# Gated heads of a hybrid encoder step: decays from a running sum along the free dimension, and a packed first stage

## The chip, the cores and the metric

One core of a Trainium2 chip runs the whole program: TensorE (PE, matmuls, with PEld for its weight loads), VectorE (DVE), ScalarE (ACT), GpSimd (POOL) and SyncE (SP, which issues most DMAs). The metric is the device time of one execution in microseconds (us); the median of the runs is compared.

## The reference, cut to what matters

One step of a two-layer encoder for 256 prompt tokens and 32 sample tokens that share the weights (T = 288 columns in all). Layer 0 mixes with four retention heads and four gated heads (GLA), layer 1 with attention; each is followed by a convolution FFN. The change touches the gated heads and the beginning of the program.

```python
z = jnp.einsum('btd,de->bte', h, w_in).astype(f32)          # h = rmsnorm(x)
qa, ka, va, ga, qb, kb, vb, gb, lo = jnp.split(z, cuts, axis=-1)
...
log_a = (jax.nn.log_sigmoid(lo @ gate_w2 + gate_b) / GLA_GATE_TAU).reshape(B, T, H_GLA, DK_GLA)
...
def gla_chunk(S, q, k, v, log_a):
    b = jnp.cumsum(log_a, axis=1)
    diff = b[:, :, None] - b[:, None, :]
    w = jnp.where(causal, jnp.exp(jnp.where(causal, diff, 0.0)), 0.0)
    scores = jnp.einsum('bihd,bjhd,bijhd->bhij', q, k, w)
    o = jnp.einsum('bhij,bjhv->bihv', scores, v)
    o = o + jnp.einsum('bihd,bhdv->bihv', q * jnp.exp(b), S)
    b_last = b[:, -1]
    S_new = jnp.exp(b_last)[..., None] * S + jnp.einsum('bjhd,bjhv->bhdv', k * jnp.exp(b_last[:, None] - b), v)
    return S_new, o
```

The gate has rank 16 (`lo`), 4 heads of 128 features, and a divisor of 16 under the exponent.

## The kernel before

**Layout and matmuls.** Features lie on the 128 partitions and the 288 tokens along the free dimension, so an activation of 2048 features is 16 tiles of 128 x 288. Weights and activations are f32; each is split into a rounded part and a rest (`wh`, `wl`, `xh`, `xl`), and a product is three matmuls (L81 to L83: high by high, high by low, low by high). One input product (`input_product`, L76) is 16 k-tiles times three matmuls, 48 of 288 columns, into one PSUM tile `acc` (four of them). Its weights come in two halves of 128 x 1024 (512 KB) on SP's queue (L58), four such buffers `w`; ScalarE casts each half (L59), VectorE subtracts (L60), three buffers each. Small matmuls use four PSUM tiles `mm`.

**Order.** A framework orders the instructions: each engine gets its own in-order list, filled by priority (program order) and by what the planner holds ready. So an instruction may run ahead of others that stand before it in the code, on engines that have nothing ready; on the chip every engine then works through its list in order.

**Start** (`start`, L244). `first_project` (L85) loads x in four pieces and the key weights of gated head 0 in two, all on SP's queue; per k-tile `gain_in` (L137) makes `xh` on ScalarE and `xl` on VectorE, and three matmuls follow. Then come the low-rank product (L254 to L266: weights of 16 columns, split by ScalarE and VectorE into one padded 128-column tile, 32 matmuls) and the query product of head 0. x's squares are summed meanwhile (L101); `norm_stat` (L158) turns the sums into R, the reciprocal root mean square of every token, spread over all partitions (L162 to L188: six tiny matmuls, a chain of small VectorE and ScalarE operations, six more matmuls). R is multiplied into every product when it leaves PSUM.

**Gates** (`gates`, L424). Tokens on partitions: three matmuls of the scaled `lo` (33 rows, the last for the bias) with the gate weights, 512 columns, f32; then Abs, Exp and Ln on ScalarE (L433 to L437), a minimum and subtraction on VectorE (L439), and a split into `la` (L440). They run after the first value product v0 of head 0.

**A gated head** (`gla_head`, L465). k, q, v0, v1 and two gate products z0, z1 (head 0 has k and q from the start). Scores inside the chunk are built in seven levels (128, 64, ... 2): at each level the second half of a block looks back at the first, with decays counted to the middle of the block. The decays of all levels and of the chunk ends are sums over `log_a`: L487 multiplies `la` (128 tokens x 128 features) with `lvl`, a constant 0/1 matrix per level, in 14 matmuls per head and five PSUM tiles, and ScalarE takes the Exp from PSUM into E (128 x 9 x 288, one buffer; L493 to L507). Then VectorE multiplies k and q by E (L525), small matmuls form the masked scores (L536), VectorE merges them (L545, L564), and outputs, states and the head's norm follow (L569 to L596). Heads are chained so that the next head's products fill TensorE between the small matmuls (`chain`, L227). `lvl` is loaded once on SP's queue and rounded (L409 to L413).

**Memory.** Pool "in" holds x and the low-rank weights during the start; pools "b" (36,928 bytes a partition) and "ab" (everything of the mixer) are opened after it and take its place, b first, from the same address on.

## Time and profile before

| what | us |
|---|---|
| median of 3 runs (2724.24 to 2726.68) | 2724.97 |
| the profiled execution | 2725.65 |
| its span, first to last instruction | 2723.9 |
| TensorE busy | 2699.6 |
| VectorE busy | 1559.9 |
| ScalarE busy | 1118.2 |
| GpSimd busy | 117.9 |

The span is what the trace shows; the time of the execution has 1.75 us around it. Busy time of PE counts overlapping matmuls once, and a matmul's end is modelled; where two matmuls follow each other without a wait, the distance of their starts is what one costs. In a timeline row stand start, duration, engine, line, operation, the tiles (written <- read), the shapes, the count of merged instructions, and in brackets how long the engine had been idle before and what released it. A row of a group has busy time, mean duration in ns, and idle time before its instructions.

### The profile page before, as it was taken

Reading aid. Unit: us, or ns where it says so; the run is one execution under the profiler, and the core shown is the slowest. Engines: PE = TensorE matmul, PEld = TensorE weight load, DVE = VectorE, ACT = ScalarE, POOL = GpSimd, SP = SyncE. Lnnn points to the kernel's source line nnn. Section 1 sums busy time; section 2 is a strip of 40 time slices with the busy share of each in tenths; the row PEclk is TensorE's granted clock in tenths of the full one; section 3 lists DMA queues with packets and bytes.
Section 4 is the critical chain, followed back from the end, with each engine's and each line's share of the span. In section 5 each row is a group of like instructions: output and inputs, shape, how many; then the busy total and the mean of one; then the engine's idle time right before and its main releaser. Section 6 shows DMA issues by size and latency. Waiting matters only on the chain.

```text
span 2723.9 us, 48869 instructions
## 1 busy us (share of the span) xinstructions
PE 2699.6 (99%) x20240; PEld 2667.4 (98%) x20240; DVE 1559.9 (57%) x2496; ACT 1118.2 (41%) x1494; POOL 117.9 (4%) x428
## 2 busy tenths in 40 slices
PE   8999999999999999999999999999999999999998
PEld 7999999999999999999999999999999999999998
DVE  5566555666665446666555555556666544666544
ACT  7444344443333333434444444444433333433443
POOL 1000000000000000000001110000000000000000
PEclk9999999999999999999999999999999999999999
DMA  5344444555555555555556555544555555555554
GB/s 197 117 134 137 155 155 151 192 163 166 167 165 163 167 171 164 169 164 164 166 174 205 186 184 169 164 158 163 169 164 168 162 165 171 166 167 165 164 167 130
DMA packets 126911, 448.81 MB, mean 165 GB/s; under 512 B 15866, under 2 KB 16186, under 8 KB 126688
## 3 DMA queue, kind: packets, MB, share of 16 engines
q1 hardware_dynamic: 119664, 427.15, 49.5%
q0 software_dynamic: 6880, 18.50, 2.1%
q8 instruction: 158, 2.59, 0.4%
q14 instruction: 65, 0.53, 0.1%
q10 hardware_dynamic: 144, 0.04, 0.0%
HBM read 435.22 MB, written 10.40 MB: 164 GB/s over the span
## 4 chain that ended last, share of the span: by engine, by line
PE 98%; ACT 1%; DVE 1%; DMA 0%; issue 0%; SPq 0%; DVEq 0%; ACTq 0%
PE acc L82 31%; PE acc L83 31%; PE acc L81 31%; PE mm L536 1%; DMA w<-in_w_in 0%; PE mm L382 0%; PE mm L659 0%; ACT wh L59 0%; PE mm L748 0%; PE mm L712 0%; ACT L493 0%; PE mm L660 0%; DVE wl L60 0%; PE mm L649 0%; PE mm L185 0%; PE mm L487 0%
## 5 line engine op out<-in xcount | busy, mean ns | idle before, releaser
L59 ACT CAST wh<-w 128x1024 fp32r<-128x1024 f32 (+1 forms) x816 | 844.3, 1035 | 1484.4 <-PE acc L82 1205.0
L60 DVE TENSOR_TENSOR wl<-w,wh 128x1024 fp32r<-128x1024 f32 (+1 forms) x816 | 980.6, 1202 | 747.7 <-ACT wh L59 747.3
L81 PE MATMUL acc<-xh,wh 128*128 128x288 f32 x4480 | 1323.3, 295 | 8.1 <-ACT wh L59 8.1
L83 PE MATMUL acc<-xh,wl 128*128 128x288 f32 x4480 | 1324.3, 296 | 1.3 <-DVE wl L60 1.3
L82 PE MATMUL acc<-xl,wh 128*128 128x288 f32 x4480 | 1324.7, 296 | 0.0
L81 PEld LDWEIGHTS acc<-xh,wh 128*128 128x128 f32 x4480 | 844.0, 188 | 11.9 <-ACT wh L59 8.4
L83 PEld LDWEIGHTS acc<-xh,wl 128*128 128x128 f32 x4480 | 843.2, 188 | 2.8 <-DVE wl L60 2.1
L82 PEld LDWEIGHTS acc<-xl,wh 128*128 128x128 f32 x4480 | 843.8, 188 | 2.0 <-issue 1.0
L82 PE MATMUL acc<-bl,wh 128*128 128x288 f32 x1920 | 566.0, 295 | 0.0
L83 PE MATMUL acc<-bh,wl 128*128 128x288 f32 x1920 | 565.6, 295 | 0.0
L81 PE MATMUL acc<-bh,wh 128*128 128x288 f32 x1920 | 563.6, 294 | 0.4 <-ACT wh L59 0.4
L81 PEld LDWEIGHTS acc<-bh,wh 128*128 128x128 f32 x1920 | 360.8, 188 | 1.5 <-ACT wh L59 0.6
L82 PEld LDWEIGHTS acc<-bl,wh 128*128 128x128 f32 x1920 | 360.8, 188 | 0.1
L83 PEld LDWEIGHTS acc<-bh,wl 128*128 128x128 f32 x1920 | 360.5, 188 | 0.2 <-issue 0.2
L312 DVE SCALAR_TENSOR_TENSOR gc<-gp,convp,gc 128x290 f32<-128x290 f32 x176 | 91.3, 519 | 3.2
L318 DVE TENSOR_TENSOR v<-acc,R 128x288 f32<-128x288 f32 x88 | 40.2, 457 | 87.8 <-PE acc L83 87.8
L303 DVE TENSOR_TENSOR gp<-acc,R 128x256 f32<-128x256 f32 x88 | 37.4, 425 | 88.4 <-PE acc L83 88.4
L305 POOL COPY conv_out<-gp 128x2 f32<-128x2 f32 x88 | 16.2, 185 | 1309.0 <-DVE gp L303 1309.0
L116 ACT CAST bh<-v 128x288 fp32r<-128x288 f32 x88 | 38.1, 433 | 14.6 <-DVE v L320 14.6
L310 DVE TENSOR_SCALAR gc<-gp,convp 128x290 f32<-128x290 f32 x88 | 38.0, 431 | 10.2 <-POOL conv_out L306 0.9
L319 DVE TENSOR_TENSOR v<-v,sg 128x256 f32<-128x256 f32 x88 | 37.4, 425 | 9.2
L117 DVE TENSOR_TENSOR bl<-v,bh 128x288 fp32r<-128x288 f32 x88 | 39.7, 451 | 0.7 <-ACT bh L116 0.7
(254 smaller groups left out, 1098.6 us busy)
## 6 DMA issues: line engine op xcount, KB each, us to landing
w<-in_w_ffn_up SPq DMA_DIRECT2D x352, 512.0 KB, 3.8
w<-in_w_ffn_down SPq DMA_DIRECT2D x128, 512.0 KB, 3.7
w<-in_w_in SPq DMA_DIRECT2D x112, 512.0 KB, 3.8
w<-in_w_qkv SPq DMA_DIRECT2D x96, 512.0 KB, 3.8
w<-in_w_ffn_down SPq DMA_DIRECT2D x64, 384.0 KB, 3.2
w<-in_w_out_ab SPq DMA_DIRECT2D x32, 512.0 KB, 3.9
w<-in_w_out_att SPq DMA_DIRECT2D x32, 512.0 KB, 3.8
x<-in_xT SPq DMA_DIRECT2D x4, 576.0 KB, 5.7
```

The lines of the kernel that those rows point to most:

```text
L59: nc.scalar.copy(h, w)
L60: nc.vector.tensor_tensor(l, w, h.bitcast(F32), op=ALU.subtract)
L81: nc.tensor.matmul(ps, lhsT=h, rhs=xh, start=first, stop=False)
L82: nc.tensor.matmul(ps, lhsT=h, rhs=xl, start=False, stop=False)
L83: nc.tensor.matmul(ps, lhsT=l, rhs=xh, start=False, stop=last)
L116: self.nc.scalar.copy(h, v)
L117: self.nc.vector.tensor_tensor(l, v, h.bitcast(F32), op=ALU.subtract)
L303: nc.vector.tensor_tensor(gp[:, 2 : TP + 2], g[:, :TP], self.R[:, :TP], op=ALU.mult)
L310: nc.vector.tensor_scalar(gc, gp[:, 0:W], cw[:, 0:1], cw[:, 3:4], op0=ALU.mult, op1=ALU.add)
L312: nc.vector.scalar_tensor_tensor(gc, gp[:, w : w + W], cw[:, w : w + 1], gc, op0=ALU.mult, op1=ALU.add)
L318: nc.vector.tensor_tensor(v, u, self.R, op=ALU.mult)
L319: nc.vector.tensor_tensor(v[:, :TP], v[:, :TP], s[:, :TP], op=ALU.mult)
```

## The change

1. **Gates with features on partitions.** `gates` multiplies the gate weights (as the stationary operand, 128 columns per head) with `lo`: four matmuls of 288 columns, in two groups, head 0 first and then heads 1 to 3, each group with its own Abs, Exp, Ln and subtraction. A `tensor_tensor_scan` per group forms running sums along the tokens; `keep` is 1 except for 0 at tokens 0, 128 and 256, where the sum starts anew.
2. **Decays from differences.** In each gated head, the 14 matmuls with `lvl` and the Exp from PSUM go. VectorE forms, per level, (sum at the middle) - (sum) for first halves and (sum) - (sum at the middle) for second halves, and three differences to the ends of the token blocks; ScalarE takes Exp(x/16) from E to E in five calls.
3. **Packed first stage.** x, the key and query weights of head 0 and the low-rank weights are packed by k-tile into one array (128 x 16 x 560) and loaded in nine chunks (1, 1, then 2 k-tiles each) on SP's queue. Per k-tile eight matmuls are issued: three for k0, three for q0, two for the low-rank product. The low-rank split moves to GpSimd, the identity's load to SP, ten matmuls of ones go ahead, and one dummy activation asks for ScalarE's table.
4. **Order around the norm.** v0's product is issued ahead of the squares and the norm; the first half of v1, in a tile of the small PSUM pool, between the norm's sums and its spread (`norm_sums` is cut into `norm_sums` and `norm_spread`); the second half after the gates.

The core of the diff:

```diff
+        cuts = (0, 1, 2, 4, 6, 8, 10, 12, 14, 16)
+
+        for _ in range(10):
+            nc.tensor.matmul(self.mm()[:, :P], lhsT=self.ones, rhs=self.ones, start=True, stop=True)
+        for c, (i, j) in enumerate(zip(cuts, cuts[1:])):
+            n = j - i
+            nc.sync.dma_start(xw[:, i:j, :], src[:, i:j, :])
...
+            for k in range(i, j):
                 self.gain_in(k, 0)
-                self.passes(ps, h[:, j, :], l[:, j, :], self.xh[k], self.xl[k], k == 0, k == KD - 1)
+                if k == i:
+                    if c:
+                        nc.scalar.copy(h, w)
+                    else:
+                        nc.vector.tensor_copy(h, w)
+                    nc.vector.tensor_tensor(l, w, h.bitcast(F32), op=ALU.subtract)
+                    nc.gpsimd.tensor_copy(lo[:, :, :RANK], wlo)
+                    nc.gpsimd.tensor_tensor(
+                        lo[:, :, RANK : 2 * RANK], wlo, lo[:, :, :RANK].bitcast(F32), op=ALU.subtract
+                    )
...
+                for o in range(N_FIRST):
+                    nc.tensor.matmul(ps[o], lhsT=h[:, at, o, :], rhs=self.xh[k], start=first, stop=False)
+                for o in range(N_FIRST):
+                    nc.tensor.matmul(ps[o], lhsT=h[:, at, o, :], rhs=self.xl[k], start=False, stop=False)
+                for o in range(N_FIRST):
+                    nc.tensor.matmul(ps[o], lhsT=l[:, at, o, :], rhs=self.xh[k], start=False, stop=last)
+                nc.tensor.matmul(ps[-1], lhsT=lo[:, at, :], rhs=self.xh[k], start=first, stop=False)
+                nc.tensor.matmul(ps[-1], lhsT=lo[:, at, :], rhs=self.xl[k], start=False, stop=last)
+            if j == 12:
+                self.first_square(xw[:, :, :T], 0)
...
+        nc.scalar.activation(self.R[:, :1], self.ones[:, :1], AF.Square)
+        xw = self._one(pool, "xw", [P, KD, T + N_FIRST * P + RANK])
...
+        lo_h = self._one(pool, "lo_h", [P, KD, P], None, F32R)
+        nc.gpsimd.memset(lo_h.bitcast(F32)[:, :, 2 * RANK :], 0.0)
+        k0, q0, lo_ps = self.first_products(a["x_first"], xw, lo_h)
+        self.ident = self.const("ident", [P, P], F32, a["ident"], nc.sync)
+        v0 = self.input_product(w[VB])
         self.first_squares(x_in)
-        self.ident = self.const("ident", [P, P], F32, a["ident"])
-        self.norm_stat()
-        return k0, q0, lo_ps
+        d = self.norm_sums()
+
+        v1 = self.mm()[:, :T]
+        second = lambda part: self.project(w[VB + 1], self.xh, self.xl, KD, chunks=(0, WCH), part=part, ps=v1)
+        second(0)
+        nc.scalar.copy(self.R, self.norm_spread(d))
+        return k0, q0, v0, lo_ps, second
...
-        la = [one("lah", [P, 3, 512], None, F32R), one("lal", [P, 3, 512], None, F32R)]
-        lvl = one("lvl", [P, 9, P], None, F32R)
-        for i, n in ((0, 8), (8, 1)):
-            f = self.wp.tile([P, WCH, P], F32, name="w", tag="w", bufs=4)[:, :n, :]
-            nc.sync.dma_start(f, a["lvl"][:, i : i + n, :])
-            nc.scalar.copy(lvl[:, i : i + n, :], f)
+        sums = one("sums", [P, H_GLA, T])
+        keep = one("keep", [P, H_GLA, T])
+        nc.gpsimd.memset(keep, 1.0)
+        for t in (0, P, TP):
+            nc.gpsimd.memset(keep[:, :, t : t + 1], 0.0)
...
+            for i, j in ((0, 1), (1, H_GLA)):
+                x = pool.tile([P, H_GLA, T], F32, name="lg", tag="lg", bufs=1)[:, i:j, :]
+                ps = []
+                for h in range(i, j):
+                    ps.append(self.mm()[:, :T])
+                    nc.tensor.matmul(ps[-1], lhsT=w2[:, h * P : (h + 1) * P], rhs=lo, start=True, stop=True)
+                    nc.scalar.activation(x[:, h - i, :], ps[-1], AF.Abs)
                 nc.scalar.activation(x, x, AF.Exp, scale=-1.0)
...
+                nc.vector.tensor_tensor_scan(
+                    flat(sums[:, i:j, :]), flat(keep[:, i:j, :]), flat(x), 0.0, op0=ALU.mult, op1=ALU.add
+                )
...
-        for t in range(2):
-            c = slice(t * P, (t + 1) * P)
-            ps = self.mm()
-            decay(ps, t, P, lvl[:, 0:4, :])
-            nc.scalar.activation(E[:, 0:4, c], ps.rearrange("p (l t) -> p l t", l=4), AF.Exp)
...
+        for i, l in enumerate(LEVELS):
+            n = T if l <= TS else TP
+            x, e = halves(b[:, :n], l), halves(E[:, i, :n], l)
+            mid = x[:, :, 0, l // 2 - 1 : l // 2].to_broadcast([P, n // l, l // 2])
+            between(e[:, :, 0, :], mid, x[:, :, 0, :])
+            between(e[:, :, 1, :], x[:, :, 1, :], mid)
+            if i == 1:
+                decay(E[:, 0:2, :TP], E[:, 0:2, :TP])
+        decay(E[:, 2:7, :], E[:, 2:7, :])
+        decay(E[:, 7, P:], b[:, P:])
+        for out, n, end in ((E[:, 7, :P], 0, P), (E[:, 8, P:TP], P, TP), (E[:, 8, TP:], TP, T)):
+            between(out, b[:, end - 1 : end].to_broadcast([P, end - n]), b[:, n:end])
+        decay(E[:, 7, :P], E[:, 7, :P])
+        decay(E[:, 8, P:], E[:, 8, P:])
```

More of the change, by code (lines that the diff above doesn't have):

```diff
@@ L26 @@
 RANK = 16
+N_FIRST = 2
 WCH = 8
@@ L112, in mm, with first_square @@
+        for c in range(4, KD, 4):
+            self.first_square(x, c)
+            nc.vector.tensor_tensor(x[:, 0:4, :], x[:, 0:4, :], x[:, c : c + 4, :], op=ALU.add)
+        nc.vector.tensor_tensor(x[:, 0:2, :], x[:, 0:2, :], x[:, 2:4, :], op=ALU.add)
+        nc.vector.tensor_tensor(x[:, 0, :], x[:, 0, :], x[:, 1, :], op=ALU.add)
+        self.ssq = x[:, 0, :]
+    def first_square(self, x, c):
+        self.nc.scalar.activation(x[:, c : c + 4, :], x[:, c : c + 4, :], AF.Square)
     def mm(self):
@@ L453, in ab_mixer @@
         heads = [
-            self.gla_head(pool, hd, w, la, lvl, masks, eyem, hg, (k0, q0, gates) if hd == 0 else None)
+            self.gla_head(pool, hd, w, sums, masks, eyem, hg, (k0, q0, v0, gates, second) if hd == 0 else None)
             for hd in range(H_GLA)
@@ L463, in _one, with gla_head @@
         return t
-    def gla_head(self, pool, hd, w, la, lvl, masks, eyem, hg, first):
+    def gla_head(self, pool, hd, w, sums, masks, eyem, hg, first):
         nc, a = self.nc, self.a
@@ L833, in _constants @@
     s, t = np.arange(P)[:, None], np.arange(P)[None, :]
-    lvl = np.zeros((P, 9, P), f32)
     masks = np.zeros((P, 7, 64), np.uint32)
@@ L838, in _constants @@
         behind = t >= mid
-        lvl[:, i] = np.where(behind, (s >= mid) & (s <= t), (s > t) & (s < mid))
         m = (s // l == t // l) & (s < mid) & behind
         masks[:, i] = m[:, behind[0]]
-    lvl[:, 7] = s <= t
-    lvl[:, 8] = s > t
-    c["lvl"], c["masks"] = lvl / f32(16.0), masks
+    c["masks"] = masks
     lg = np.log1p(-(2.0 ** (-5.0 - np.arange(H_RET))))
```

110 lines of the change are left out of this document (36 added, 74 removed).

## The prediction

> **What bounds the kernel now.** I read the page first, then the stretch up to 275 us (start and gated heads, the only part that the change touches) in the timeline, engine by engine, then the windows of that stretch, the chain of waits, and the groups by line with shapes kept apart. Page:
>
> ```profile
> span 2723.9 us, 48869 instructions
> PE 2699.6 (99%) x20240; PEld 2667.4 (98%) x20240; DVE 1559.9 (57%) x2496; ACT 1118.2 (41%) x1494; POOL 117.9 (4%) x428
> PE 98%; ACT 1%; DVE 1%; DMA 0%; issue 0%; SPq 0%; DVEq 0%; ACTq 0%
> ```
>
> TensorE is busy for the whole span and the chain that ends last is 98% PE. So a removed matmul is worth its full step on PE, and work put on VectorE or ScalarE costs nothing until PE has to wait for it. What is left to gain beside matmuls is the few microseconds in which PE waits or runs slowly, at the start (timeline, PE and ScalarE; start and duration in us):
>
> ```profile
> 3.92 1.28 ACT L140 ACT_TABLE_LOAD   x1 [3.92 <-DMA x_in<-in_xT]
> 7.18 0.61 PE L81 MATMUL acc<-xh,wh 128*128 128x288 f32 x1 [7.18 <-ACT wh L59]
> ...
> 10.97 0.44 PE L81 MATMUL acc<-xh,wh 128*128 128x288 f32 x1
> 11.21 0.44 PE L82 MATMUL acc<-xl,wh 128*128 128x288 f32 x1
> ...
> 13.05 0.29 PE L81 MATMUL acc<-xh,wh 128*128 128x288 f32 x1
> 13.18 0.29 PE L82 MATMUL acc<-xl,wh 128*128 128x288 f32 x1
> ...
> 14.96 0.41 PE L81 MATMUL acc<-xh,wh 128*128 128x288 f32 x1 [0.96 <-ACT wh L59]
> ...
> 31.38 0.59 PE L170 MATMUL mm<-ones,x_in 128*96 128x1 f32 x6
> 31.83 0.38 PE L81 MATMUL acc<-xh,wh 128*128 128x288 f32 x1
> ```
>
> Durations overlap, so I go by the step from start to start. A 288-column matmul steps by 0.24 us at first (10.97 to 11.21) and by 0.13 from 13.05 on. More exactly 48 x 0.1315 = 6.3 us for one input product. The first stage (two input products and the low-rank one, 48 + 48 + 32 = 128 matmuls) ends at 31.38, where the norm's sums begin. At the fast step it is 128 x 0.1315 = 16.8 us. So 31.38 - 16.8 = 14.6 us of it are start, half-rate steps and waits.
>
> **First stage.** The first rows of x land at 3.9 (the table load that waits for them starts at 3.92); then come that load, 1.28, a cast of 1024 columns and the first matmul at 7.18. The new code issues the table load before any data, casts 256 columns on VectorE instead, and fills PE from about 1.0 us with ten matmuls of 128 x 128 in f32. Their price comes from a row of the chain:
>
> ```profile
> 1443.31 0.43 PE mm L712 x2
> ```
>
> One f32 matmul of 256 columns is two records, 0.43 us; one of 128 columns is thus about 0.22, and ten are 2.2 us at the fast step, 4.4 at half rate: PE is free of them between 3.2 and 5.4. The first packed chunk (one of 16 rows, 0.29 MB, like the 0.29 MB that landed at 3.9) is ready with gain, cast and subtraction, about 0.5 us each and partly side by side, at about 4.9. I take 5.2 for the first real matmul, 2.0 us earlier than now. From there 16.8 us give 22.0.
>
> Whether the data keep up is read from the windows (PE, PEld, DVE, ACT, POOL busy with counts, then clock, DMA share, GB/s):
>
> ```profile
> 2.00:18.00 16.00, 8.72 (x34) 7.29 (x35) 8.76 (x17) 10.67 (x21) 7.12 (x15) 0.95 1.01 364
> 31.38:66.23 34.85, 33.23 (x226) 29.72 (x225) 20.38 (x36) 26.40 (x36) 0.00 (x0) 1.00 0.43 144
> ```
>
> The DMA engines are full from 2 to 18 us and move 364 GB/s. The packed input is 128 x 16 x 560 x 4 bytes = 4.59 MB; GpSimd's loads beside it are about 1.0 MB. At 364 GB/s the 5.6 MB are there at 2 + 15.4 = 17.4 us, and the last chunk needs about 1.2 us of preparation and 16 matmuls, 2.1 us: 20.7. So the matmuls end last, not the loads; early chunks of two rows (0.57 MB, 1.6 us) come about as fast as PE eats them (2.1 us). SP's queue also loses the two level-matrix loads, which held it today:
>
> ```profile
> 8.41 8.10 SPq L412 DMA_DIRECT2D w<-in_lvl  x2
> 23.18 45.83 SPq L58 DMA_DIRECT2D w<-in_w_in  x15
> ```
>
> Weights for v0 can be issued right behind the packed chunks and the identity (64 KB), so they land by about 21, before v0 starts. I add 1.0 us for short waits and a piece at half rate: **23.0 instead of 31.38, -8.4 us**.
>
> [...]
>
> **Norm, gates and the first head's products.** From 31.38 to the first head's transposes (66.23):
>
> ```profile
> 36.94 0.40 ACT L160 COPY R<-mm 128x288 f32<-128x288 f32 x1 [0.69 <-PE mm L185]
> 39.77 2.95 PE L432 MATMUL mm<-w,lo 33*128 33x512 f32 x6
> 45.48 1.28 ACT L437 ACT_TABLE_LOAD   x1
> 59.00 0.33 PE L487 MATMUL mm<-lvl,lah 128*128 128x128 f32 x1 [0.99 <-ACT E L493]
> 66.23 0.81 PE L382 MATMUL mm<-ident,v 128*128 128x128 f32 x6
> ```
>
> These 34.85 us hold four input products (25.25), norm sums and spread (0.45 + 0.69), the gates' matmuls (2.88 from start to start), the decay matmuls of L487 (3.91, of which 0.99 idle: the fifth PSUM tile waits for the Exp) and 1.67 us of waits. The new code keeps the products and the norm. The gates become four f32 matmuls of 288 columns, 2304 columns in all records instead of 3072: 2.88 x 0.75 = 2.16. L487 goes. That makes 28.55 plus waits.
>
> For the waits: all four PSUM tiles of the products are full until R exists, so PE has only v1, which sits in a tile of the small pool, to run behind the norm. That is 6.3 us in two halves; the norm's chain of small operations (31.83 to R's copy at 36.94) is about 5 us, so little is uncovered. Behind R, ScalarE is the tight engine:
>
> ```profile
> L59 ACT CAST wh<-w 128x1024 fp32r<-128x1024 f32 x752 | 790.7, 1052 | 1398.2 <-PE acc L82 1144.0 <-issue 223.3 <-PE acc L83 8.1
> L105 ACT ACTIVATE x_in<-x_in 128x1152 f32<-128x1152 f32 x4 | 4.5, 1156 | 0.0
> L368 ACT ACTIVATE gz<-gz 128x288 f32<-128x288 f32 x16 | 7.1, 444 | 0.1
> ```
>
> Between R (about 34) and the masked scores (about 54) it has four Abs (1.7), Exp and Ln in two groups of 288 and 864 columns (2 x 0.44 + 2 x 0.9), two table loads for each group and one back to Exp (5 x 1.28 = 6.4), the head's decays (about 2.8, the longest 1440 columns, sized by the 1152-column row) and six casts (6.3): 19.9 of 20 us. One wait is new: "in" grows to 44,032 bytes a partition (35,840 + 8,192), past the 36,928 of the pool that later lies there, so sums and keep share bytes with the split low-rank weights, and GpSimd's fill of keep waits for their last matmul (23.0). If the loads of masks and gate weights stand behind it, they are issued at about 25 and land by 30 to 33; the gates need them at 35. Therefore waits of 2.5 instead of 1.67: **28.55 + 2.5 = 31.05 instead of 34.85, -3.8 us**.
>
> The running sum has no row. Below it is bounded by a plain 288-column VectorE operation (0.45), above by the costliest, RECIPROCAL (1.95): 864 columns are 1.4 to 5.8 us. I take the low end, since it reads and adds like the plain one. It feeds heads 1 to 3, needed 30 us later, so even the upper end is covered there; the first head's, 288 columns, costs at most 1.5 more.
>
> [...]
>
> **Heads 1 to 3.** Each head's decay matmuls and their neighbourhood, and the first masked matmuls of heads 1, 2 and 3 in the chain:
>
> ```profile
> 103.18:107.08 3.90, 3.71 (x22) 3.01 (x20) 1.68 (x2) 3.76 (x5) 0.00 (x0) 1.00 0.53 175
> ...
> 106.31 0.33 PE L487 MATMUL mm<-lvl,lah 128*128 128x128 f32 x1 [0.19 <-ACT E L493]
> ...
> 113.56 0.62 PE mm L536 x6
> 166.53 0.62 PE mm L536 x6
> 219.48 0.62 PE mm L536 x6
> ```
>
> In the 3.90 us stand 14 decay matmuls and six weight matmuls (6 x 0.1315 = 0.8). The rest, 3.1 us, disappears: **3 x 3.1 = -9.3 us**. In their place VectorE computes differences: 14 over half the columns of a level, 3 for the ends. The same shapes are there already:
>
> ```profile
> L525 DVE TENSOR_TENSOR qk<-k,E 128x144 f32<-128x144 f32 x20 | 6.1, 304 | 6.0 <-ACT E L505 3.2 <-PE mm L536 2.8
> ...
> 69.00 0.30 DVE L525 TENSOR_TENSOR qk<-k,E 128x144 f32<-128x144 f32 x1
> 69.22 0.30 DVE L525 TENSOR_TENSOR qk<-q,E 128x144 f32<-128x144 f32 x1
> ...
> 84.00:113.00 29.00, 28.81 (x210) 28.00 (x209) 18.99 (x31) 14.63 (x20) 1.00 (x2) 1.00 0.44 141
> L127 DVE RECIPROCAL ry<-rsq 128x288 f32<-128x288 f32 x8 | 15.6, 1948 | 2.1 <-ACT rsq L126 2.1
> ```
>
> They step by 0.22, so 17 x 0.22 = 3.7 us a head. VectorE is busy 18.99 of the 29 us before a head's scores; the differences need only the sums, which exist long before, and tile E, free once the previous head's state is out. So they fit into idle VectorE time. The Exps move from PSUM to SBUF at about the same ScalarE time. I allow **+1.0 us** over the three heads for weight splits that come late behind a burst.
>
> **Sum.** -8.4 - 3.8 - 9.3 + 1.0 = -20.5 us. Against the profiled execution (2725.65 us, of which the span is 2723.9) that is 2705.15; the median of the runs is 0.7 lower, 2724.97, so the prediction is **2704.5**.
>
> **Rivals.**
>
> A. *The differences are not hidden.* If the order on VectorE leaves them until the previous head's work is done, scores wait for 3.7 us in each of three heads, and the matmuls come back as a wait: about 2704.5 - 1.0 + 11.1 = 2714.6. For it: the old decays too were computed right before use, and L525 waited for E. Against: 10 idle us of VectorE. Chance 0.13.
>
> B. *GpSimd holds the start.* It now splits the low-rank weights, and PE, in order, needs them in every row. Its queue today:
>
> ```profile
> 6.76 0.54 POOL L462 DMA_DIRECT2D kdec<-in_kdec  x1 [0.74 <-DMA wlo<-in_w_lo]
> 8.94 0.53 POOL L462 DMA_DIRECT2D qdec<-in_qdec  x1 [1.64 <-DMA ident<-in_ident]
> 10.27 0.54 POOL L601 DMA_DIRECT2D dec<-in_dec  x1 [0.80 <-DMA masks<-in_masks]
> 10.80 0.76 POOL L257 MEMSET wh<- 128x768 f32 x1
> ```
>
> Its loads wait for earlier ones to land, up to 10.27. With a fill twice as wide (1.5 us) and nine loads ahead of the first split, PE would stand from about 6 to about 11 and run at half rate behind it: +5 to +6.6, about 2710.5. Against: two of the eleven loads are gone. Chance 0.17.
>
> C. *Slower.* The differences read a broadcast column and strided halves. If each costs like RECIPROCAL per element (1948/288 = 6.8 ns, so 1.0 us for 144), a head's burst is 17 us; three weight buffers cover about 6.3, and 10.7 us a head, four times, are lost: about 2704.5 - 1 + 43 = 2746. It ends on the slower side once a difference costs over some 0.8 us; L525 with the same strides costs 0.22. Chance 0.03.
>
> D. *The gains are given back elsewhere* (A and B together, or weights late on ScalarE in the first head): 2720 to 2730, chance 0.02.
>
> **How the numbers follow.** My forecast, 2699 to 2710, has 0.60: its low end is a first stage without the 1.0 and no extra waits. Still faster, 0.05. The range 2698 to 2715 takes in the forecast, B and most of A. A measurement of this kernel tells 0.2%, 5.4 us, from no change; below 2719.5 is faster: 0.95. Within: 0.02. Slower: 0.03.
>
> **What would show it.** First real matmul at about 5, steps of 0.13 soon after; norm sums at about 23; first masked matmuls at about 55; from head to head 49.9 us instead of 52.96 (113.56 to 166.53); no decay matmul; VectorE's gaps, not PE's, taking the differences. Norm sums past 26 with PE waiting for GpSimd would be B; head distances of 53 with waits before the scores A; over 57, C.

## The result and the profile after

| | before | after |
|---|---|---|
| median of the runs, us | 2725.02 (4 runs) | 2710.66 (4 runs, 2709.72 to 2712.19) |
| ratio to before, with its 95% interval | 1 | 0.9945 (0.9933 to 0.9957) |
| profiled execution, us | 2725.65 | 2710.59 |
| its span, us | 2723.9 | 2708.8 |

The change makes the kernel 0.55% faster, 14.4 us by the medians. Forecast were 20.5, so the predicted 2704.5 lies 6.2 us below the measured median, which is inside the range of 2698 to 2715 and 0.7 above the forecast proper, 2699 to 2710. That the range holds is in part luck: its upper end was there for rivals A and B, and what filled it was neither.

The page of the changed kernel, the same three lines as before:

```profile
span 2708.8 us, 48875 instructions
PE 2690.0 (99%) x20206; PEld 2661.5 (98%) x20206; DVE 1573.9 (58%) x2568; ACT 1114.5 (41%) x1487; POOL 124.7 (5%) x447
PE 98%; ACT 1%; DVE 1%; issue 0%; DMA 0%; DVEq 0%; SPq 0%; ACTq 0%
```

TensorE is as full as it was; VectorE has 14 us more to do and nobody notices that in the shares. The difference must be looked for in places. Timeline of TensorE in the changed kernel (start and duration in us, then line, operation, tiles, shapes, and in brackets the idle time before it and what ended it). L120 to L126 are the first stage, L463 the gates, L82 to L84 the products with streamed weights, L567 the masked scores:

```profile
1.05 4.00 PE L94 MATMUL mm<-ones 128*128 128x128 f32 x20 [1.05 <-DVE ones L233]
4.81 0.52 PE L120 MATMUL acc<-xh,wh 128*128 128x288 f32 x2
...
8.50 0.53 PE L120 MATMUL acc<-xh,wh 128*128 128x288 f32 x2 [1.77 <-ACT wh L109]
...
24.18 0.29 PE L82 MATMUL acc<-xh,wh 128*128 128x288 f32 x1
...
39.16 1.69 PE L463 MATMUL mm<-lo,w 33*128 33x288 f32 x6 [1.56 <-issue]
...
42.06 0.44 PE L83 MATMUL acc<-xl,wh 128*128 128x288 f32 x1
42.30 0.44 PE L84 MATMUL acc<-xh,wl 128*128 128x288 f32 x1
...
56.65 0.41 PE L82 MATMUL acc<-xh,wh 128*128 128x288 f32 x1 [1.24 <-ACT wh L60]
...
61.15 1.11 PE L567 MATMUL mm<-qk 128*128 128x64 f32 x9
```

Three marks cut the start into pieces: the end of the first stage (the next product starts at 24.18), the first masked score of head 0 (61.15), and from there the distances from head to head. The chain of waits gives the masked scores of head 0 before, and of heads 1 to 3 after:

```profile
67.05 0.62 PE mm L536 x6
```

```profile
1.65 5.73 DMA xw<-in_x_first
...
104.96 0.62 PE mm L567 x6
154.69 0.62 PE mm L567 x6
204.42 0.62 PE mm L567 x6
```

(The chain's rows start 0.16 behind those of the timeline, before as after: head 0 of the changed kernel stands in it at 61.31.) With the rows of before that stand in the prediction:

| piece | before, us | after, us | measured | forecast |
|---|---|---|---|---|
| first stage ends | 31.38 | 24.18 | -7.2 | -8.4 |
| from there to the first masked scores | 35.5 | 37.0 | **+1.5** | **-3.8** |
| masked scores of head 0 to those of head 3 | 152.43 | 143.11 | -9.3 | -9.3, and +1.0 allowed |
| span | 2723.9 | 2708.8 | -15.1 | -20.5 |

The three heads come out to the tenth. The first stage is short by 1.2. The stretch between them was to shrink and grew. The span misses the forecast by 20.5 - 15.1 = 5.4 us, and this stretch alone by 1.5 + 3.8 = 5.3; the first stage's 1.2 is about balanced by the 1.0 that was allowed for the heads and not needed. The windows of the changed kernel (busy time of PE, PEld, DVE, ACT, POOL with counts, then granted clock, DMA share, GB/s):

```profile
2.00:12.00 10.00, 8.22 (x55) 7.77 (x54) 5.43 (x12) 6.62 (x14) 3.37 (x12) 1.00 0.99 375
24.18:61.15 36.97, 33.85 (x221) 31.28 (x220) 25.69 (x57) 25.11 (x34) 6.41 (x16) 0.91 0.44 142
41.77:48.60 6.83, 6.83 (x26) 5.80 (x25) 5.28 (x16) 5.34 (x8) 0.00 (x0) 0.50 0.24 78
```

In the stretch of 36.97 us PE is idle for 36.97 - 33.85 = 3.1 us, and for 6.83 us its granted clock is 0.50, so half of them, 3.4, are lost. The work alone, by the prediction, is the 28.55 that it named without waits and the 0.66 of the transposes ahead of the masked scores: 29.2. 29.2 + 3.1 + 3.4 = 35.7. Most of the other 1.3 us is work that the prediction had too small; the run w2_defer shows it below. What PE waited for is seen on ScalarE (L60 is the cast of streamed weights, L464 to L466 are the gates' Abs, Exp and Ln, L524 the decays):

```profile
42.05 1.03 ACT L60 CAST wh<-w 128x1024 fp32r<-128x1024 f32 x1
43.10 1.28 ACT L466 ACT_TABLE_LOAD   x1
...
46.28 1.01 ACT L464 ACTIVATE lg<-mm 128x288 f32<-128x288 f32 x3 [1.45 <-DVE sums L472]
47.32 1.28 ACT L524 ACT_TABLE_LOAD   x1
...
48.85 0.91 ACT L465 ACTIVATE lg<-lg 128x864 f32<-128x864 f32 x1
...
50.30 1.28 ACT L466 ACT_TABLE_LOAD   x1
51.59 0.93 ACT L466 ACTIVATE lg<-lg 128x864 f32<-128x864 f32 x1
52.54 1.28 ACT L524 ACT_TABLE_LOAD   x1
53.83 1.83 ACT L524 ACTIVATE E<-E 128x1440 f32<-128x1440 f32 x3
55.57 2.92 ACT L60 CAST wh<-w 128x1024 fp32r<-128x1024 f32 x3
```

Between the cast at 42.05 and the three at 55.57 there are 12.5 us without a cast. In them stand the rest of the first gate group, the decays of head 0, and the whole second gate group (864 columns, for heads 1 to 3, needed 30 us later) with two of the table loads: 1.01 + 0.91 + 0.93 + 2 x 1.28 = 5.4 us. PE waits at the end of it for wh. The other wait, before the gates at 39.16, goes back to GpSimd:

```profile
31.34 1.06 POOL L444 MEMSET keep<- 128x1152 f32 x1 [14.28 <-DVE rv L157]
...
33.14 0.55 POOL L496 DMA_DIRECT2D w<-in_w  x1
```

GpSimd's fill of keep was let go at 31.34, by the norm's sums, and not at 23.0, by the low-rank matmuls, as the prediction had it. The row names VectorE's first step of the norm (L157) as what let it go, long after the low-rank matmuls. That the start's buffers are freed only together, by the last reader of any of them, fits this, but no run tests it. So the load of the gate weights went out at 33.14 and landed at 38.97.

### The profile page after: what moved, and what is told of

The parts are those of the page before. It is cut to its first block, busy times and chain, and to the rows that moved or that the text cites. A ratio compares the mean times of both kernels' runs of the same rounds, so it can differ in the third digit from the quotient of the medians.

```text
span 2708.8 us, 48875 instructions
## 1 busy us (share of the span) xinstructions
PE 2690.0 (99%) x20206; PEld 2661.5 (98%) x20206; DVE 1573.9 (58%) x2568; ACT 1114.5 (41%) x1487; POOL 124.7 (5%) x447
## 4 chain that ended last, share of the span: by engine, by line
PE 98%; ACT 1%; DVE 1%; issue 0%; DMA 0%; DVEq 0%; SPq 0%; ACTq 0%
PE acc L83 31%; PE acc L84 31%; PE acc L82 31%; PE mm L567 1%; PE mm L415 0%; PE mm L690 0%; PE mm L779 0%; PE mm L743 0%; ACT wh L60 0%; DMA xw<-in_x_first 0%; PE mm L691 0%; DVE wl L61 0%; PE mm L680 0%; DVE y L375 0%; PE mm L742 0%
## 5 line engine op out<-in xcount | busy, mean ns | idle before, releaser
L60 ACT CAST wh<-w 128x1024 fp32r<-128x1024 f32 (+1 forms) x812 | 839.7, 1035 | 1465.8 <-PE acc L83 1198.4
L83 PE MATMUL acc<-xl,wh 128*128 128x288 f32 x4432 | 1309.7, 296 | 0.0
L84 PE MATMUL acc<-xh,wl 128*128 128x288 f32 x4432 | 1309.2, 295 | 0.3 <-DVE wl L61 0.3
L82 PE MATMUL acc<-xh,wh 128*128 128x288 f32 x4432 | 1308.1, 295 | 1.2 <-ACT wh L60 1.2
L82 PEld LDWEIGHTS acc<-xh,wh 128*128 128x128 f32 x4432 | 834.6, 188 | 3.3 <-ACT wh L60 1.5
L83 PEld LDWEIGHTS acc<-xl,wh 128*128 128x128 f32 x4432 | 834.4, 188 | 1.9 <-issue 1.3
L84 PEld LDWEIGHTS acc<-xh,wl 128*128 128x128 f32 x4432 | 833.6, 188 | 1.6 <-issue 0.8
L84 PE MATMUL acc<-bh,wl 128*128 128x288 f32 x1920 | 565.6, 295 | 0.0
L82 PE MATMUL acc<-bh,wh 128*128 128x288 f32 x1920 | 563.6, 294 | 0.4 <-ACT wh L60 0.4
L82 PEld LDWEIGHTS acc<-bh,wh 128*128 128x128 f32 x1920 | 360.8, 188 | 1.5 <-ACT wh L60 0.6
L84 PEld LDWEIGHTS acc<-bh,wl 128*128 128x128 f32 x1920 | 360.5, 188 | 0.2 <-issue 0.2
```

The costliest lines, as they stand in the source:

```text
L60: nc.scalar.copy(h, w)
L82: nc.tensor.matmul(ps, lhsT=h, rhs=xh, start=first, stop=False)
L83: nc.tensor.matmul(ps, lhsT=h, rhs=xl, start=False, stop=False)
L84: nc.tensor.matmul(ps, lhsT=l, rhs=xh, start=False, stop=last)
```

## The experiments

Two theories for the stretch between the first stage and the first masked scores:

- **Theory 1**: the late load of the gate weights makes PE idle at 37.6, the clock halves behind that, and the rest follows.
- **Theory 2**: ScalarE has too much to do ahead of head 0's decays, the second gate group above all; the casts of the weights come late, whatever else is cured.

All experiments start from the changed kernel, if nothing else is said. The table has their positions by the timeline, in us: first stage's end, first masked scores of head 0, and the distances to those of heads 1, 2, 3. The ratios are to the kernel before, run on the same chip.

| run | median, us | ratio (95%) | first stage | head 0 | to 1 | to 2 | to 3 |
|---|---|---|---|---|---|---|---|
| before | 2725.02 | 1 | 31.38 | 66.89 | 46.51 | 52.96 | 52.96 |
| after | 2710.66 | 0.9945 (0.9933 to 0.9957) | 24.18 | 61.15 | 43.65 | 49.73 | 49.73 |
| w2early | 2710.45 | 0.9943 (0.9930 to 0.9955) | 24.20 | 60.35 | 43.64 | 49.74 | 49.74 |
| defer | 2709.09 | 0.9938 (0.9926 to 0.9951) | 24.54 | 54.37 | 49.71 | 49.74 | 49.74 |
| w2_defer | 2708.30 | 0.9936 (0.9922 to 0.9949) | 23.65 | 52.05 | 48.19 | 49.74 | 49.73 |
| w2_perhead | **2703.65** | **0.9920 (0.9905 to 0.9934)** | 23.69 | 52.10 | 44.25 | 50.65 | 50.66 |
| w2_mid | 2704.47 | 0.9922 (0.9908 to 0.9935) | 23.11 | 51.52 | 45.92 | 49.73 | 49.73 |
| chunks | 2711.62 | 0.9948 (0.9934 to 0.9962) | 24.16 | 62.39 | 43.65 | 49.73 | 49.75 |
| nowarm | 2711.69 | 0.9949 (0.9936 to 0.9962) | 26.18 | 62.74 | 43.64 | 49.74 | 49.75 |
| twice | 2713.50 | 0.9956 (0.9943 to 0.9969) | 24.32 | 64.36 | 43.70 | 49.87 | 49.75 |
| decays_only | 2713.01 | 0.9952 (0.9939 to 0.9964) | 29.53 | 64.26 | 43.29 | 49.74 | 49.75 |
| start_only | 2720.50 | 0.9987 (0.9978 to 0.9996) | 24.00 | 60.82 | 46.52 | 52.95 | 52.96 |
| after_again | 2711.63 | 0.9949 (0.9936 to 0.9961) | 24.33 | 64.69 | 43.63 | 49.74 | 49.75 |

### w2early: the gate weights are loaded at the start

```diff
+        self.w2 = self.const("w2", [2 * RANK + 1, 512], F32, a["w2"], nc.sync)
...
-        w2 = one("w2", [2 * RANK + 1, 512], a["w2"])
+        w2 = self.w2
```

> Only the place of the gate weights changes: they lie in the constant pool and are loaded on SP's queue behind the identity, so they are there at about 18 us instead of 38.97. In the changed kernel PE stood idle from 37.60 to 39.16 before the gates' matmuls (L463) and ran at half rate from about 41.8 to 48.5. Theory 1 (the late loads cost the time: the wait and the half rate that follows it): the gates' matmuls start at about 37.6, no half-rate stretch, and the first masked matmul comes at 56 to 57.5 instead of 61.15; about 2706. Theory 2 (ScalarE's list, with five table loads and the second gate group ahead of the casts, ends the stage whatever PE does): the first masked matmul moves only by the 1.6 us that the gates start earlier, to about 59.5; about 2709.

The idle time before the gates is gone, and the time is the same as after: 2710.45 against 2710.66. Timelines of TensorE and ScalarE of this run (line numbers one higher than in the changed kernel):

```profile
55.07 0.61 PE L82 MATMUL acc<-xh,wh 128*128 128x288 f32 x1 [4.28 <-ACT wh L60]
```

```profile
40.47 1.03 ACT L60 CAST wh<-w 128x1024 fp32r<-128x1024 f32 x1
...
53.99 2.92 ACT L60 CAST wh<-w 128x1024 fp32r<-128x1024 f32 x3
```

PE reaches the wait for the cast earlier, at 50.79, and waits there 4.28 us instead of 1.24. ScalarE's list again has 12.5 us without a cast; it starts and ends 1.6 us earlier. The masked scores come at 60.35, 0.8 later than theory 2 had them: behind this longer wait the clock is halved from 54.58 to 57.99, which takes 1.7 us of PE's time. Theory 1 falls as the cause of the loss; the load was a wait in front of another wait.

### defer: the second gate group is issued at the end of head 0

```diff
-        def gates():
-            for i, j in ((0, 1), (1, H_GLA)):
+        def gates(part):
+            for i, j in (((0, 1), (1, H_GLA))[part],):
...
-            first[3]()
+            first[3](0)
...
+        if first:
+            first[3](1)
```

> The second gate group (heads 1 to 3) is issued at the end of head 0 instead of in the middle of its values. The gate weights stay late. Theory 1: the idle time before the gates and the half rate stay; only the 1.24 us in which PE waits for a cast at 55.41 goes: first masked matmul at about 59.5, about 2709. Theory 2: ScalarE is rid of 5.3 us (three Abs, Exp, Ln of 864 columns and two table loads) before the scores; casts come in time, first masked matmul at 56 to 57, about 2706. If the group then stands in the way of head 1, the distance from head 0 to head 1 grows by some of it.

Windows and the timelines of TensorE and VectorE (L472 the scan, L521 the differences, L432 the value's scaling):

```profile
30.89:54.37 23.48, 22.07 (x167) 21.24 (x166) 16.89 (x47) 18.05 (x23) 6.43 (x16) 1.00 0.49 160
...
85.00:90.00 5.00, 5.00 (x40) 5.00 (x39) 5.00 (x10) 3.99 (x5) 0.00 (x0) 1.00 0.38 121
...
95.00:100.00 5.00, 4.19 (x19) 3.91 (x20) 5.00 (x12) 2.89 (x7) 0.00 (x0) 0.66 0.49 151
```

```profile
95.12 0.55 PE L415 MATMUL mm<-ident,v 128*128 128x128 f32 x3 [1.65 <-DVE v L432]
...
96.36 0.45 PE L84 MATMUL acc<-xh,wl 128*128 128x288 f32 x1 [0.69 <-DVE wl L61]
```

```profile
80.77 1.95 DVE L472 TENSOR_TENSOR_SCAN sums<-keep,lg 128x864 f32<-128x864 f32 x1
...
93.34 1.36 DVE L521 TENSOR_TENSOR E<-sums 128x144 f32<-128x144 f32 x6
94.62 0.45 DVE L432 TENSOR_TENSOR v<-acc,R 128x288 f32<-128x288 f32 x1
```

Theory 2 is right about the first head: its masked scores come 6.8 us earlier (54.37 against 61.15), more than the 56 to 57 that was expected. Not all of it is ScalarE's: the idle time before the gates is still there (1.38 us), but the clock is 1.00 all through, and with the 3.4 us that the half rate took in the changed kernel the scores would come at about 57.8. Why the clock did not fall here is open (see chunks); and three heads' gate matmuls, some 1.65 us of PE's work (see w2_defer), have also moved out of the stretch. But only some 1.6 us of it arrive in the time (2709.09, where 2706 was expected), because the next distance grows from 43.65 to 49.71. The sums of heads 1 to 3 now exist only at 82.7, VectorE is full from 85 on (5.00 of 5.00 us), and the differences of head 1 run ahead of the scaling of its value, for which PE stands 1.65 us, then 0.69 for a weight split; behind that the granted clock drops to 0.66. This is the prediction's rival A, the differences that are not hidden, in a kernel that calls for them too late. w2_defer shows it again.

### w2_defer: both together

The edits of w2early and defer in one kernel.

> Both edits. Theory 1 and theory 2 are additive if each stands for a part: first masked matmul at about 54 to 55, close to the 54.05 of the prediction's sum for this stage, and about 2703.5 to 2705. If one of them alone makes up the loss, this run equals the better of the two single edits within 1 us.

With ScalarE freed, the early load is worth 54.37 - 52.05 = 2.3 us at this place, 0.9 of them from the first stage. Both waits are gone: the window of the stretch has PE busy all through and the clock at 1.00.

```profile
23.65:52.05 28.40, 28.36 (x214) 27.58 (x213) 22.05 (x53) 19.81 (x25) 5.83 (x15) 1.00 0.57 183
```

These 28.4 us hold the gate matmuls of head 0 only. In w2early six of the eight gate matmuls, as many as three heads have, take 39.20 - 37.55 = 1.65 us of PE from start to start, so the change's work in this stretch, with all four heads' gates, is about 28.4 + 1.65 = 30.05, where the prediction's sum makes it 29.2: 0.85 too little. With it the stretch of the changed kernel comes to 30.05 + 3.1 + 3.4 = 36.6 of the 36.97 measured. The next distance is again long, 48.19, with the same wait for v (1.65 us), so the time, 2708.30, misses the 2703.5 to 2705 that was expected, although the place is better than expected. The late load does count, but only once ScalarE's list is not behind it.

### w2_perhead and w2_mid: the second group in the middle of head 0

Early load of the gate weights, as in w2early, and each head's gates as a group of their own, those of head h + 1 behind the masked scores of head h:

```diff
-            for i, j in ((0, 1), (1, H_GLA)):
+            for i, j in ((g, g + 1),):
...
+        if hd + 1 < H_GLA:
+            gates(hd + 1)
```

> Gate weights early as before; each head's gate is a group of its own, and head h+1's group is issued in head h after its masked scores, when ScalarE was busy for 1.3 us out of 5. In the run that issued the second group at the end of head 0, PE lost the gain of the first head again at 93 to 99 us, where VectorE was full (the sums came at 82.7, so the differences stood in front of the scaling of v1, and the transposes of v1 waited 2.3 us, with half rate after it). If that lateness is the cause, sums that come about 8 us earlier keep the gain: first masked matmuls of heads 0 and 1 at about 52 and 96, about 2703.5. If ScalarE's two more table loads a head (2.6 us each) end the stages instead, the distance of the heads grows above 49.7: about 2708 or more.

```diff
...
+        if first:
+            first[3](1)
```

w2_mid puts the undivided group of heads 1 to 3 at that same place in head 0.

> As the run with a group per head, but heads 1 to 3 in one group, issued in head 0 after its masked scores: four table loads fewer than with a group per head. If the 0.9 us by which each head's distance had grown there (50.65 instead of 49.73) is the price of the small groups, the distances are 49.7 here and the time is about 2702. If three gate tiles out of the four of the small PSUM pool, held until Ln is done, stop the next small matmuls, the first distance grows by 2 to 5 us: 2705 to 2708.

The window of w2_perhead from the masked scores of head 0 to those of head 1:

```profile
52.10:96.35 44.25, 44.25 (x324) 41.81 (x323) 33.58 (x89) 28.00 (x42) 1.61 (x5) 1.00 0.43 142
```

PE is not idle at all from head 0 to head 1 (44.25 of 44.25 us at clock 1.00), and the gain of the first head stays. Every distance is 0.6 to 0.9 longer than after; the gate matmul of the next head, 62.20 - 61.52 = 0.68 from start to start in this run, is most of it. Three heads so give back about 2.4 of the 9.0 us by which head 0 is earlier. The time is 2703.65, 7.0 under the changed kernel's, and the intervals against before (0.9905 to 0.9934, and 0.9933 to 0.9957) overlap by 0.0001. w2_mid pays its gate matmuls once, in a distance of 45.92, and comes to 2704.47, between its two expectations; the two runs cannot be told apart. w2_mid's interval ends at 0.9935, and that of after_again, which ran beside it on the same chip, begins at 0.9936. So both stand below both given kernels, against the changed one by little more than the noise, and both lie where the prediction put the change.

### chunks: the third packed chunk in two

```diff
-        cuts = (0, 1, 2, 4, 6, 8, 10, 12, 14, 16)
+        cuts = (0, 1, 2, 3, 4, 6, 8, 10, 12, 14, 16)
```

> The changed kernel with the third packed chunk cut in two (1, 1, 1, 1, then 2 k-tiles each). In the changed kernel PE finished the first two k-tiles at 6.72 and stood until 8.50, because the third chunk, 0.57 MB, landed only at 7.38. If the size of that chunk is the cause, PE's idle time there shrinks from 1.8 us to under 1 and the 128 matmuls of the first stage end at about 23.0 to 23.4 instead of 24.18. If the DMA rate of the first microseconds is the limit whatever the chunks are, they end within 0.3 us of 24.18. In the time little of it may be left, since ScalarE's list in the first head ends the next stage: 2709.5 to 2710.7.

TensorE's timeline:

```profile
10.05 0.54 PE L120 MATMUL acc<-xh,wh 128*128 128x288 f32 x2 [1.21 <-ACT wh L109]
```

The wait moves one chunk on and the stage ends where it did (24.16 against 24.18). The first stage is held by how much of x and its weights has landed by 8 to 10 us; this finer cut does not help. In the changed kernel the DMA engines are full (0.99, 375 GB/s in the window from 2 to 12 above): by 7.38, when the third chunk is there, they have moved 7.38 x 262 GB/s (the mean from 0 to 7.38) = 1.9 MB, where the first four rows are 4 x 0.29 = 1.15 MB. Beside the chunks only the gains and the identity, 0.1 MB, were issued by then; the first weights of v0 went out at 7.39. So chunks that are needed later took a share of the engines from those needed first.

The time, 2711.62, lies above the 2709.5 to 2710.7 that was expected, and the first masked scores come 1.2 later than in the changed kernel. A window behind the gates has a longer half rate than there:

```profile
39.65:49.89 10.24, 10.24 (x36) 8.15 (x35) 5.88 (x18) 7.27 (x11) 0.00 (x0) 0.50 0.29 96
```

Here the clock is halved for 10.24 us, behind an idle time of only 1.36 us before the gates. In defer 1.38 us at the same place brought nothing. So the length of the idle time alone does not decide.

### nowarm: without the ten matmuls at the start

```diff
-        for _ in range(10):
-            nc.tensor.matmul(self.mm()[:, :P], lhsT=self.ones, rhs=self.ones, start=True, stop=True)
```

> The changed kernel without the ten f32 matmuls of ones at the start. If they bring the fast step early, the first stage runs at 0.24 us a step for the first 3 to 6 us without them and ends 1.5 to 3 us after 24.18. If the data's arrival would hide the slow steps anyway (PE waits until 8.5 for the third chunk), it ends within 0.5 us of 24.18.

TensorE's timeline of this run; a row of two matmuls takes 0.85 here where it takes 0.52 in the changed kernel:

```profile
4.51 0.85 PE L118 MATMUL acc<-xh,wh 128*128 128x288 f32 x2 [4.51 <-DVE wl L110]
```

Without the ten matmuls the half rate lasts until about 12.5 us (with a wait of 1.17 in it) and the stage ends 2.0 later, at 26.18, as expected if they bring the fast step early. The time is 1.0 longer by the medians, which the intervals do not separate.

### twice: every difference formed twice

```diff
-            nc.vector.tensor_tensor(out, a, b, op=ALU.subtract)
+            for _ in range(2):
+                nc.vector.tensor_tensor(out, a, b, op=ALU.subtract)
```

> Every difference of the gated heads is formed twice by VectorE (the same values written again): 17 more operations a head, 3.7 us of VectorE each. If the differences of heads 1 to 3 lie in idle VectorE time, the distance between the first masked matmuls of heads 1, 2 and 3 stays at 49.73 us, and only the first head grows, by up to 3.7 us: 2710.7 to 2714. If they are on the path or close to it, each distance grows by 1 to 3.7 us: 2714 to 2725.

VectorE's and TensorE's timelines in the first head, and the window from head 1 to head 2:

```profile
45.70 3.67 DVE L522 TENSOR_TENSOR E<-sums 128x128 f32<-128x128 f32 x17
...
55.37 3.17 DVE L522 TENSOR_TENSOR E<-sums 128x144 f32<-128x144 f32 x15
```

```profile
59.73 0.61 PE L84 MATMUL acc<-xh,wl 128*128 128x288 f32 x1 [5.26 <-DVE wl L61]
```

```profile
108.05:157.92 49.87, 49.87 (x369) 47.66 (x368) 38.05 (x106) 24.78 (x38) 1.59 (x5) 1.00 0.41 138
```

In heads 1 to 3 some 3.6 us of added VectorE work a head change the distances by 0.05, 0.14 and 0.02: the differences are hidden there, with room for as many again. The first head is 3.2 us later (64.36 against 61.15), within the 3.7 that was expected. A second execution of the unchanged kernel (after_again, below) has 64.69 there, but for another reason: here the clock does not fall behind the gates. Instead PE stands 5.26 us for a split of weights, which VectorE, busy for 7.96 of the 8 us from 52 to 60, starts only at 58.47, behind the second batch of differences. So in the first head the added differences are on the path. How much of the 3.2 is theirs is not separated, since ScalarE's casts also stand in another order in this run.

### decays_only and start_only: the halves of the change

decays_only is the kernel before with the running sums, the gates by features and the differences of the change, and the old start. start_only is the changed kernel with the old gates, level matrices and decay matmuls put back:

```diff
-        sums = one("sums", [P, H_GLA, T])
-        keep = one("keep", [P, H_GLA, T])
...
+        la = [one("lah", [P, 3, 512], None, F32R), one("lal", [P, 3, 512], None, F32R)]
+        lvl = one("lvl", [P, 9, P], None, F32R)
...
+            decay(ps, t, P, lvl[:, 0:4, :])
```

> The kernel before with the gates by scan and the decays from differences, and the old first stage and old order around the norm. It keeps the old memory of the start (19,456 bytes a partition, under the 36,928 of the pool behind it), so GpSimd's loads go out at once. If heads 1 to 3 gained by the missing matmuls alone, they take 49.7 us each here too (52.96 before), and the norm's sums start at 31.4. In the first head the gates cost ScalarE four table loads as in the changed kernel: if ScalarE is what ends that stage, the stage gains nothing and the time is about 2715.5; if the loads and the half rate were the cause, it gains 3 to 4 us and the time is about 2712.

> The changed kernel with the old gates and the old decay matmuls: the packed first stage and the order around the norm alone. Heads 1 to 3 take 52.96 us each again. The new first stage puts the end of its 128 matmuls at 24.2 instead of 31.38, 7.2 us earlier. If the first head can use that, the time is about 2718; if its ScalarE work and the late loads (gate weights, and now the level matrix on SP's queue, all behind the release of the start's memory) eat it, the time is 2722 or more.

Head 0's masked scores in the chain of each, decays_only first:

```profile
64.42 0.62 PE mm L533 x6
```

```profile
60.99 0.62 PE mm L570 x6
```

Against the 67.05 of before, the decays alone bring the first masked scores 2.6 forward, the start alone 6.1, and both together 5.7 (61.31). Behind that point the decays bring the distances down by 9.6 alone and 9.3 in the change, the start alone by nothing. So the halves add up in heads 1 to 3, and in the first head they do not.

The table tells more of the first head when the first stage's end is taken off. The stretch behind it is 35.5 us before, 64.26 - 29.53 = 34.7 in decays_only, 60.82 - 24.00 = 36.8 in start_only and 37.0 in the change. So the new gates and decays save 0.8 there behind the old start and nothing behind the new one, which alone makes the stretch 1.3 longer. The other 1.9 of decays_only's 2.6 is its first stage, which ends earlier (29.53 against 31.38); why is open. In decays_only GpSimd issues the load of the gate weights at 4.09, and PE still waits 2.13 us for a cast, at 54.63: theory 2 again, with the old start. Of start_only the trace shows the fastest of 11 executions (2719.29, the slowest is 2726.24), so its places are its best. Both times lie between their two expectations.

By the medians beside them the decays are worth 12.6 us and the start 5.2 (its interval reaches from 1 to 6), together 17.8, of which the change has 14.4; with these intervals the difference is not clear of the noise.

### after_again: the changed kernel once more

> The changed kernel once more beside these: 2710 to 2711.5 by its earlier runs. It says how far the version with a group per head (2703.65) and the one with one later group stand below it on the same chip.

The median is 2711.63, just above what was expected, that of the first runs 2710.66. The profiled execution was a longer one, 2713.44, and shows where the executions of one kernel differ:

```profile
40.06:50.30 10.24, 10.24 (x34) 8.08 (x33) 5.79 (x16) 6.91 (x10) 0.00 (x0) 0.50 0.28 91
60.50:63.91 3.41, 3.41 (x16) 3.41 (x15) 3.12 (x6) 2.28 (x5) 0.00 (x0) 0.51 0.59 179
```

After the idle time before the gates (1.79 us here) the clock is halved for 10.24 us, in the first profile for 6.83, and a second time, for 3.41, behind the wait for the cast. That wait is 1.27 us here and 1.24 in the first profile, where the clock does not fall behind it. All distances from head to head are the same to 0.02. Against the 30.05 us of work (see w2_defer) the first head's waits and half rate thus cost between 7 and 10 us from one execution to the next.

## Why the prediction was right, and where it was wrong

- **What bounds the kernel**: right. TensorE stayed at 98% of the chain, removed matmuls were paid by their steps, and VectorE's added work cost nothing outside the first head.
- **First stage, 23.0**: right in kind, mis-sized by 1.2. The first real matmul came at 4.81 (5.2 forecast), at the fast step almost from the beginning. The term "I add 1.0 us for short waits and a piece at half rate" was an estimate that no run shows; in its place the runs have 24.18 - 4.81 - 16.8 = 2.6, of which the earlier start gave 0.4 back: one wait of 1.77 for the third chunk, whose load took 5.73 us (the first row of the chain; 1.6 for one chunk of two rows was forecast). The sum of bytes was right for the end of the stage and wrong for its first 8 us, because it let the chunks land one after the other; cutting that chunk in two did not mend it.
- **Price of the warm-up matmuls**: 2.2 to 4.4 forecast, 4.00 measured, and they were nearly free ahead of the data (the first real matmul comes at 4.51 without them, at 4.81 with them). nowarm has them worth 2.0 us of the stage.
- **Norm, gates and the first head, "waits of 2.5 instead of 1.67"**: this is the step that failed, by 5.3 us, and with it nearly all the error. The waits with the half rate behind them are 36.97 - 30.05 = 6.9, 4.4 more than the 2.5, and the work itself is 0.85 more. The prediction counted ScalarE's work between R and the masked scores at "19.9 of 20 us" and went on as if a full engine were no wait. It was a sum over the stretch; what PE needs is the casts in time within it. The planner put the second gate group and its table loads in front of three casts. w2early, defer and w2_defer show it: without the late load alone 0.8 us is gained at the place and nothing in the time, without the second group alone 6.8 at the place (3.4 of them by a clock that did not fall), without both the stretch takes 28.4 and is free of waits. The half rate is the part of the step that the sum had no term for at this place.
- **GpSimd's fill of keep, freed at 23.0**: wrong, 31.34; the argument looked at the bytes that are shared with the low-rank weights, and the fill was let go by the norm, 7 us after their last use. This error alone has no price that can be measured (w2early); where ScalarE doesn't hide it, it is 54.37 - 52.05 less the 0.9 of the first stage, 1.4 us (w2_defer against defer).
- **The scan**: the two rows on VectorE

```profile
45.43 0.76 DVE L472 TENSOR_TENSOR_SCAN sums<-keep,lg 128x288 f32<-128x288 f32 x1
46.22 3.59 DVE L521 TENSOR_TENSOR E<-sums 128x128 f32<-128x128 f32 x17
...
54.02 1.95 DVE L472 TENSOR_TENSOR_SCAN sums<-keep,lg 128x864 f32<-128x864 f32 x1
```

  give (1.95 - 0.76) / (864 - 288) = 2.07 ns an element. I took the low end, 0.45 and 1.4; it is 0.3 more in the first head. A plain operation steps by (0.45 - 0.30) / (288 - 144) = 1.04 ns an element (the rows of L432 in defer and of L525 in the prediction), so the scan takes twice that.
- **Heads 1 to 3, -9.3**: right, -9.3. The 17 differences took 3.59 us (3.7 forecast). The added 1.0 for late weight splits was not needed: PE's distances are free of waits.
- **Rival A**, differences not hidden: not in heads 1 to 3 of the change (twice), but real in the first head once there are twice as many (twice), and in head 1 once the sums come late (defer). **Rival B**, GpSimd holding the start: it did not happen; the first low-rank matmul stands in PE's list only at 11.98, behind the rows that it belongs to, and PE never waited for GpSimd there. **Rival C**: a difference costs 0.21 us, far from 0.8. **Rival D**: nothing was given back beyond the first head.

The half rate followed idle times of 1.56 us (after), 1.79 us (after_again) and 1.36 us (chunks) before the gates. Behind the bubble of 1.56 in after it cost 3.4 us of TensorE's time on top of the 1.56.

## What to carry to other kernels

When work is moved ahead of a dependency, list in order what each engine issues between the two ends, not only the sum of it: here ScalarE, with 19.9 of 20 us by the sum, kept PE waiting 1.24 us for a cast in the middle (4.28 in w2early), and table loads, which belong to no line of the mathematics, took 5.1 of the 12.5 us without a cast. A group that is wanted later should go behind the first work that is wanted now, yet early enough that its consumer on the next engine still finds idle time; here the middle of the head was right, and its beginning and its end were both wrong. Curing the wait that is seen first can be worth nothing, because another stands behind it; try the two cures apart and together.

## What the runs showed of the hardware

- A short idle time could cost more behind it than it took (1.56 us and then 3.4 in after), and the cost came in pieces of one size. Behind waits of TensorE (in w2early at the end of one) the granted clock was 0.50 for 3.41 us (before from 16.34, w2early from 54.58, decays_only from 55.9, defer from 96.5), 6.83 us (after from 41.77) or 10.24 us (after_again from 40.06, chunks from 39.65): one, two or three times 3.41, each of which took 1.7 us of full rate.
- How long the idle time was did not tell whether such a piece came. Before the gates 1.36 us (chunks) brought one and 1.38 (defer) none; before the cast 1.27 (after_again) brought one and 1.24 (after) none. It began 2.6 us behind the idle time in after, 0.5 in after_again and 0.7 in chunks. Gate matmuls, which use 33 of 128 rows, were not needed for it (in w2early none stand behind the wait for the cast, which ends at 55.07), and without idle time they did not bring it (w2early, clock 1.00 from 36 to 51). What decides stays open.
- Two profiled executions of the changed kernel have their first masked scores at 61.15 and 64.69, 3.5 us apart, almost all of it behind such waits; that is more than several of the edits are worth. Edits of the first head are better judged by their places in the trace than by the time.
- Each change between Exp and Ln had a table load of its own, 1.28 us, four of them in the ScalarE rows of the changed kernel above, 5.1 us in 12.5.
- Loads issued one behind the other on one queue did not land one after the other at the full rate: the third chunk was there at 7.38, when 1.9 MB had been moved (262 GB/s from 0 to 7.38), with 1.15 MB up to its end.
